# Last tile's first LayerNorm affine moved to VectorE in two halves, and the first expert's low parts and index work re-ordered

## The chip, the cores and the metric

The kernel runs on one core of a Trainium2 chip. The metric is the device time of one execution in microseconds (us), as the median of several runs. Beside it stands one execution taken by the hardware profiler; all rows of the trace below are of that one.

## The reference

Two decoder layers over 512 tokens of width 1024. Each layer does a mixer (attention of two kinds), adds it to alpha times its input and normalises; then a mixture of 16 experts, adds and normalises again:

```python
x = layer_norm(ALPHA * x + mix, ln_g[l, 0], ln_b[l, 0])
ffn = routed_moe(x, router_w, router_b, moe_w_gate[l], moe_w_up[l], moe_w_down[l])
x = layer_norm(ALPHA * x + ffn, ln_g[l, 1], ln_b[l, 1])
```

The router takes a sigmoid of 16 logits, picks the best group of four experts, and in it the two best experts of each token. An expert is `(silu(x @ w_gate) * (x @ w_up)) @ w_down` with an inner width of 512, weighted by the token's gate.

## The kernel before, in words

Tokens are worked in four tiles of 128. A product in float32 is done as three products of split operands: each operand is a high part (a cast on ScalarE, line 185) and a low part (a subtraction on VectorE, line 186, or for activations 203 and 204), and `mm3` multiplies high by high, high by low and low by high. A weight tile of 1 MB is two units, each with one cast and one subtraction of 128x1024. There are four buffers for high parts and four for low parts (pool `hl`).

The stage that the diff touches lies between a layer's mixer and its experts, in `out_proj` and at the head of `moe`. `ROUTE_ORDER` gives its order: `y` is the output projection of a tile and its sums (`tile_y`), `l` its LayerNorm statistics, its router logits and its normalise (`tile_ln`), and `rab` routes the tiles a to b-1. So `r02` routes tiles 0 and 1 together, `r23` tile 2, `r34` tile 3. Routing is `choose` (lines 418 to 454, a chain of small VectorE instructions, from the sigmoid `aff` to the one-hot `O` and the mask `M`), then `slots` (matmuls at 471 and 475 count the tokens ahead of each in its expert's list; 477 and 479 on VectorE make the slot numbers `sl` and the one-hot `oh0` of expert 0), then `first_rows` (line 490: 16 matmuls per tile gather the rows of expert 0 into two PSUM banks, transposed, `ps2[0]` and `ps2[1]`, lines with ps_o and ps_s).

The normalise of a tile is on ScalarE (line 589). Its scale and bias, `affine` (lines 255 and 256), are on GpSimd, but for the last 256 columns of tile 3, which VectorE does (`LN1_DVE`). The result x1 is written to HBM twice by GpSimd's DMA queue (591 to `x1d`, from which the experts' rows are gathered, and 594 to `yd`, onto which their outputs are added).

At the head of `moe`, 16 weight tiles of 1 MB are fetched ahead by the SP queue in the order `AHEAD`, into buffers named by `slot_of`; some are those of the mixer's outputs (`eH`, `eL`, `lH`, `lL`). A later load waits until the tile that was in its buffer has been split. Then come the high and low parts of expert 0's gate weights (`g0`), `put_rows` (it splits the rows from PSUM into `gH` and `gL`, which lie in `m2`), and `after_slots`. That makes each slot's token index (`idx`, line 507, with eight masks and eight matmuls at 505 and 506), masks and transposes for the end of the layer (512 to 514), counts (517, 518), the gate weights (`weights`) and each slot's gate (527 to 529). Indirect DMAs gather the rows of the other experts (`gather`, line 1100), 96 rows each. The loop over 16 experts does the gate product, the up product, the activation, the transposes of the next expert's rows (`rows_in`, line 1111) and the down product of the expert before. Expert 1's gate product needs `rows_in(1)`, since `gH` and `gL` exist once.

The order of instructions on an engine is a scheduler's, made at compile time: by the order written, among those which it takes to be ready. `keep_in_program_order` pins an instruction behind the one written before it on its engine. `issue_after(x)` queues what its block writes on x's engine behind x. Neither adds a wait on another engine. `first` pins only while `in_order[0]` is set.

Of the kernel before, what the change touches and what calls it, by code (L numbers as in the profile page):

```python
# [9 lines left out]
F32 = mybir.dt.float32  # L10
# [6 lines left out]
ALU = mybir.AluOpType  # L17
# [24 lines left out]
AHEAD = (2, 3, 4, 0, 1, 5, 6, 8, 9, 10, 12, 13, 7, 14, 11, 15)  # L42


LN1_DVE = (0, 0, 0, 256)
# [22 lines left out]
def trunk_kernel(ctx: ExitStack, tc, x_in, even_w_in, even_b_f, even_sinks, odd_w_in,  # L68
# [344 lines left out]
    def choose(t0, t1):  # L413
# [40 lines left out]
        V.tensor_tensor(out=M[:, ts_], in0=O[:, ts_, 0, :], in1=O[:, ts_, 1, :], op=ALU.add)  # L454
# [27 lines left out]
    def first_rows(ps2, oh0, t0, t1):  # L482

        for c in range(2):
# [8 lines left out]
    def after_slots(sl, oht, flag):  # L493
# [13 lines left out]
        V.tensor_scalar(idx[:CAP], sp[:CAP, 0:NE], OOB, None, op0=ALU.add)  # L507

# [10 lines left out]
        weights()  # L519

        og = sm.tile([128, NT * 2, NE], F32, name="og", tag="gt", bufs=1)
        V.tensor_tensor(out=og, in0=O.rearrange("p t c e -> p (t c) e"),
                        in1=gates.rearrange("p t c -> p (t c)").unsqueeze(2).to_broadcast([128, 8, NE]), op=ALU.mult)
        sg = ps_t()
        for j in range(NT * 2):
            eq = sm.tile([128, CAP], F32, name="eq")
            V.tensor_scalar(eq, slot1, pos[:, j:j + 1], None, op0=ALU.is_equal)
            T.matmul(sg[:CAP, 0:NE], eq, og[:, j, :], start=(j == 0), stop=(j == NT * 2 - 1))
        A.activation(out=gslot[:CAP], in_=sg[:CAP, 0:NE], func=AF.Copy, scale=1.0 / ALPHA)
# [17 lines left out]
    def out_proj(l, chunk_src, oH, oL, g, x1d, yd, work, main):  # L547
# [35 lines left out]
        def tile_ln(i):  # L583
# [5 lines left out]
            A.activation(out=xr[i], in_=xr[i], func=AF.Identity, scale=rs, bias=minus(mv[:, 0, 0:1], rs))  # L589
            affine(xr[i], gb, bb, LN1_DVE[i])  # L590
# [11 lines left out]
        for f, *n in ROUTE_ORDER.split():  # L602
            i = int(n[0])
            if f == "y":
                tile_y(i)
            elif f == "l":
                tile_ln(i)
            else:

                j = int(n[1])  # L610
                if i == 0:
                    ps2 = [ps_o(), ps_s()]
                choose(i, j)
                slots(sl, oh0, i, j)
                first_rows(ps2, oh0, i, j)
        return sl, ps2, oht
# [433 lines left out]
    def moe(l, mo, sl, ps2, oht, x1d, yd, flag, following, finish):  # L1050
# [22 lines left out]
        def fetch(t, w, e, c, chain=False):  # L1073
# [6 lines left out]
            elif t in "eElx":  # L1080
                t = xo.tile([128, 2048], F32, name="wraw3", tag=dict(e=eH, E=eL, l=lL, x=lH)[t])
# [48 lines left out]

        def act(g, u, n=1):
# [3 lines left out]
            for j in range(n):  # L1135
                cs = slice(j * FF // n, (j + 1) * FF // n)
                V.tensor_tensor(out=sg[:, cs], in0=sg[:, cs], in1=u[j], op=ALU.mult)
# [52 lines left out]
        for c in range(2):  # L1190
# [170 lines left out]
    def layer(l, proj, x1d, yd, following, finish):  # L1361
        with tc.tile_pool(name="mo", bufs=1, reuse_waits="tile") as mo:
            sl, ps2, oht = out_proj(l, *proj, x1d, yd, mo, True)
            moe(l, mo, sl, ps2, oht, x1d, yd, flags[:, l:l + 1], following, finish)
# [42 lines left out]
```

## Time and profile before

| what | value |
|---|---|
| median of three runs | 1181.48 us (1177.25 to 1182.6) |
| profiled execution | 1180.26 us, span 1178.5 us |
| TensorE (PE) busy | 1093.0 us, 93% |
| VectorE (DVE) busy | 934.3 us, 79% |
| ScalarE (ACT) busy | 762.3 us, 65% |
| GpSimd (POOL) busy | 266.5 us, 23% |
| mean granted TensorE clock | 0.954 |

The span runs from the first to the last instruction. Times in rows are from its start. PEld is TensorE's loading of stationary operands; SP is the engine whose queue issues the weight loads, and q behind an engine's name stands for its sequencer. In a timeline a row has the start, the duration, engine, line, operation, what it writes and reads, how many alike in a row, and in brackets the idle time of the engine before it with what ended it. Layer 0's routing lies between 224 and 286 us, layer 1's between 814 and 874 us.

### The profile page before, as it was taken

To read this page: it belongs to the slowest core of one execution; us is meant where nothing else is said; L and a number is where in the kernel's file an instruction comes from. 1 tells how busy PE (TensorE), PEld (TensorE's weight loads), DVE (VectorE), ACT (ScalarE), POOL (GpSimd) and SP (SyncE) were. 2 spreads that over 40 slices of the span, in tenths; PEclk is the share of its full clock that TensorE was granted. 3 is DMA by queue.
4 is the path that set the end of the run, shared out by engine and by line. 5 is a ranking of instruction groups with operands and counts; after the bars stand their busy time and mean duration, and the time that the engine had idled before them with its cause. 6 is when DMAs were issued, how large, how long until landed. Compare 5 with 4: busy or idle time off the path is not lost. (4 is left out here: it accounts for less than half of the span.)

```text
span 1178.5 us, 16701 instructions
## 1 busy us (share of the span) xinstructions
PE 1093.0 (93%) x5775; PEld 817.5 (69%) x5775; DVE 934.3 (79%) x1866; ACT 762.3 (65%) x1229; POOL 266.5 (23%) x223
## 2 busy tenths in 40 slices
PE   8999989979999999998599898999799999999982
PEld 7786767867777777776377665777677777777761
DVE  4646756597999999987766998766879999999976
ACT  4556646235888888887435744654268888888862
POOL 2001340251111141112613133003411111411023
PEclk9999999988999999999699998999789999999997
DMA  8314332779999997998512211335699999989972
GB/s 209 117 40 90 75 88 105 255 276 303 302 358 357 350 334 237 361 357 279 183 28 72 73 37 37 107 108 209 240 299 285 365 342 353 339 255 366 371 234 108
DMA packets 139613, 262.25 MB, mean 223 GB/s; under 512 B 11831, under 2 KB 28247, under 8 KB 139520
## 3 DMA queue, kind: packets, MB, share of 16 engines
q1 hardware_dynamic: 129232, 234.62, 57.9%
q0 software_dynamic: 10288, 26.48, 9.1%
q8 instruction: 47, 0.77, 0.3%
q14 instruction: 46, 0.38, 0.1%
HBM read 246.73 MB, written 22.30 MB: 228 GB/s over the span
## 5 line engine op out<-in xcount | busy, mean ns | idle before, releaser
L186 DVE TENSOR_TENSOR wl<-wraw,wh 128x1024 fp32r<-128x1024 f32 (+1 forms) x418 | 503.6, 1231 | 83.3 <-ACT wh L185 74.9
L185 ACT CAST wh<-wraw 128x1024 fp32r<-128x1024 f32 (+3 forms) x436 | 445.7, 1039 | 155.0 <-PE ps_s L200 63.8
L198 PE MATMUL ps_s<-wh,m 128*96 128x512 f32 (+1 forms) x528 | 208.3, 394 | 1.7 <-ACT m L203 1.7
L199 PE MATMUL ps_s<-wl,m 128*96 128x512 f32 (+1 forms) x528 | 206.4, 391 | 0.0
L200 PE MATMUL ps_s<-wh,m 128*96 128x512 f32 (+1 forms) x528 | 205.0, 388 | 0.4 <-DVE m L204 0.4
L200 PEld LDWEIGHTS ps_s<-wh,m 128*96 128x96 f32 x528 | 86.4, 164 | 35.7 <-DVE m L204 1.3
L198 PEld LDWEIGHTS ps_s<-wh,m 128*96 128x96 f32 x528 | 86.7, 164 | 34.8 <-ACT m L203 2.1
L199 PEld LDWEIGHTS ps_s<-wl,m 128*96 128x96 f32 x528 | 86.4, 164 | 31.9 <-issue 0.2
L198 PE MATMUL ps_a<-wh,hH 128*96 128x512 f32 x256 | 102.7, 401 | 3.8 <-ACT hH L203 3.8
L199 PE MATMUL ps_a<-wl,hH 128*96 128x512 f32 x256 | 101.8, 398 | 4.0 <-POOL wl L186 4.0
L200 PE MATMUL ps_a<-wh,hL 128*96 128x512 f32 x256 | 101.0, 394 | 1.3 <-DVE hL L204 1.3
L198 PE MATMUL ps_a<-wh,XH 128*128 128x512 f32 (+2 forms) x224 | 89.4, 399 | 4.3 <-ACT wh L185 3.2
L1100 POOL DMA_INDIRECT m<-x1d,idx x30 | 33.1, 1104 | 255.8 <-PE ps_t L1111 224.2
L200 PE MATMUL ps_a<-wh,XL 128*128 128x512 f32 (+2 forms) x224 | 88.7, 396 | 1.9 <-DVE XL L204 1.9
L1175 POOL DMA_INDIRECT yd<-m,idx x30 | 49.2, 1640 | 177.0 <-ACT m L1174 173.3
L199 PE MATMUL ps_a<-wl,XH 128*128 128x512 f32 (+2 forms) x224 | 88.8, 396 | 0.0
L199 PE MATMUL ps_a<-XL,wh 128*128 128x512 f32 x160 | 65.0, 406 | 0.0
L200 PE MATMUL ps_a<-XH,wl 128*128 128x512 f32 x160 | 64.7, 405 | 0.3 <-DVE wl L186 0.3
L198 PE MATMUL ps_a<-XH,wh 128*128 128x512 f32 x160 | 64.6, 403 | 0.0
L357 ACT ACTIVATE p<-p,nm 128x256 f32<-128x256 f32 (+3 forms) x96 | 50.6, 529 | 17.8 <-DVE nm L350 8.8
L376 ACT COPY pT<-ps_t 128x512 f32<-128x512 f32 (+2 forms) x88 | 43.4, 517 | 28.8 <-PE ps_t L373 28.0
L199 PEld LDWEIGHTS ps_a<-wl,hH 128*96 128x96 f32 x256 | 41.3, 161 | 20.5 <-POOL wl L186 5.4
(327 smaller groups left out, 1918.3 us busy)
## 6 DMA issues: line engine op xcount, KB each, us to landing
wraw<-in_moe_w_up_dram SPq DMA_DIRECT2D x64, 1024.0 KB
wraw<-in_moe_w_gate_dram SPq DMA_DIRECT2D x64, 1024.0 KB
wraw<-in_moe_w_down_dram SPq DMA_DIRECT2D x64, 1024.0 KB
wraw<-in_w_o_dram SPq DMA_DIRECT2D x6, 1024.0 KB
wraw<-in_even_w_in_dram SPq DMA_DIRECT2D x4, 1024.0 KB
x1d<-xr POOLq DMA_DIRECT2D x8, 512.0 KB
yd<-xr POOLq DMA_DIRECT2D x8, 512.0 KB
xr<-yd SPq DMA_DIRECT2D x8, 512.0 KB
```

The source lines that it names most:

```text
L185: first(A.copy(hv, w))
L186: first(eng.tensor_tensor(out=lv, in0=w, in1=hv.bitcast(F32), op=ALU.subtract))
L198: T.matmul(o, lh, rh, start=first, stop=False)
L199: T.matmul(o, lh, rl, start=False, stop=False)
L200: T.matmul(o, ll, rh, start=False, stop=last)
L357: A.activation(out=pt[h], in_=(pt if bias else Sp)[h], func=AF.Exp, bias=nm[:, h:h + 1], scale=(slopes[0][h] if slopes else 1.0), accum_ou ...
L376: A.copy(d_, s_)
L1100: G.indirect_dma_start(out=xg_of[e], out_offset=None, in_=x1d[:, :], in_offset=bass.IndirectOffsetOnAxis(ap=idx[:CAP, e:e + 1], axis=0), b ...
L1175: G.indirect_dma_start(out=yd[:, :], out_offset=bass.IndirectOffsetOnAxis(ap=idx[:CAP, e:e + 1], axis=0), in_=yos[e % 2], in_offset=None, ...
```

## The change

Tile 3's scale and bias move from GpSimd (768 columns) and VectorE (256) to VectorE alone, in halves of 512 columns: the first behind its choice, the second behind its one-hot `oh`, where `first_rows` is split in two as well. The writes of x1 of tile 3 move behind that. The normalise of every tile is pinned behind its sigmoid. The first expert's gate weights are split behind the last one-hot and in a written order: first half, both `put_rows`, second half. What `after_slots` did for expert rows and gates is written behind the first gate product; what it did for the layer's end becomes `for_the_end`, written in expert 4 behind the activation of expert 3. Buffers change places: `m2` lies in `lL`, and `m3` and the weight tile of place 7 (expert 1's up, second half) in `eL`, whose first tenant is the second half of the first gate; that weight tile is fetched last of the 16.

```diff
-AHEAD = (2, 3, 4, 0, 1, 5, 6, 8, 9, 10, 12, 13, 7, 14, 11, 15)
+AHEAD = (2, 3, 4, 0, 1, 5, 6, 8, 9, 10, 12, 13, 14, 11, 15, 7)
-LN1_DVE = (0, 0, 0, 256)
+LN1_DVE = (0, 0, 0, 1024)
...
-    def affine(x, gb, bb, nv):
+    def affine(x, gb, bb, nv, half=None):
         for e, cs in ((G, slice(0, D - nv)), (V, slice(D - nv, D))):
-            if cs.start < cs.stop:
+            if half is not None:
+                cs = slice(half * 512, half * 512 + 512)
+            if cs.start < cs.stop and (half is None or e is V):
...
-            A.activation(out=xr[i], in_=xr[i], func=AF.Identity, scale=rs, bias=minus(mv[:, 0, 0:1], rs))
-            affine(xr[i], gb, bb, LN1_DVE[i])
+            tc.keep_in_program_order(A.activation(out=xr[i], in_=xr[i], func=AF.Identity, scale=rs, bias=minus(mv[:, 0, 0:1], rs)))
+            if i < NT - 1 or not main:
+                x1(i, True)
...
-                choose(i, j)
-                slots(sl, oh0, i, j)
-                first_rows(ps2, oh0, i, j)
+                chosen = choose(i, j)
+                if j < NT:
+                    slots(sl, oh0, i, j)
+                    first_rows(ps2, oh0, i, j)
+                    continue
+                with tc.issue_after(chosen.ins):
+                    affine(xr[i], gb, bb, D, 0)
+                oh = slots(sl, oh0, i, j)
+                first_rows(ps2, oh0, i, j, (0,))
+                with tc.issue_after(oh.ins):
+                    affine(xr[i], gb, bb, D, 1)
+                first_rows(ps2, oh0, i, j, (1,))
+                x1(i)
...
-                m3 = xo.tile([128, 2, D], F32, name="m3", tag=lL)
+                m3 = xo.tile([128, 2, D], F32, name="m3", tag=eL)
...
-        g0 = [ksplit(load("g", 0, c), 2) for c in range(2)]
-        m2 = xo.tile([128, 2, D], F32R, name="m2", tag=eL)
+        m2 = xo.tile([128, 2, D], F32R, name="m2", tag=lL)
-        for c in range(2):
-            put_rows(c, ps2[c])
-        after_slots(sl, oht, flag)
-        for e in (1, 2):
-            gather(e)
+        with tc.issue_after(oh.ins):
+            in_order[0] = True
+            g0 = [ksplit(load("g", 0, 0), 2)]
+            for c in range(2):
+                put_rows(c, ps2[c])
+            g0.append(ksplit(load("g", 0, 1), 2))
+            in_order[0] = False
         for e in range(NE):
             g = up("g", e, None if e else g0)
+            if e == 0:
+                after_slots(sl)
+                for i in (1, 2):
+                    gather(i)
+            if e == 4:
+                with tc.issue_after(act_op[0].ins):
+                    for_the_end(sl, oht, flag)
```

## Rows read from the trace of the kernel before

**Rows 1.** The page: the busy time of each engine with its share of the span and its instructions, and the share of the chain that ended last by engine.

```profile
PE 1093.0 (93%) x5775; PEld 817.5 (69%) x5775; DVE 934.3 (79%) x1866; ACT 762.3 (65%) x1229; POOL 266.5 (23%) x223
PE 24%; DVE 2%; ACT 1%; issue 0%; POOL 0%; DVEq 0%; ACTq 0%
```

**Rows 2.** The chain that ended last, in layer 1's routing and behind it, in order of time: start, us, what.

```profile
848.93 1.86 DVE xr L256
851.11 1.99 PE ps_o L490 x8
853.10 1.71 PE ps_s L490 x8
855.76 1.99 PE ps_o L490 x8
857.75 1.71 PE ps_s L490 x8
...
876.42 0.23 PE ps_s L199
```

**Rows 3.** The timeline of VectorE in layer 1's routing.

```profile
842.98 1.21 DVE L186 TENSOR_TENSOR wl<-wraw,wh 128x1024 fp32r<-128x1024 f32 x1
...
846.80 2.05 DVE L255 TENSOR_TENSOR xr<-xr,lnt 128x256 f32<-128x256 f32 x1
...
848.89 1.91 DVE L256 TENSOR_TENSOR xr<-xr,lnt 128x256 f32<-128x256 f32 x1
...
850.88 0.16 DVE L418 TENSOR_TENSOR sel<-aff,rb 128x16 f32<-128x16 f32 x1
...
853.51 0.17 DVE L454 TENSOR_TENSOR M<-O 128x16 f16<-128x16 f16 x1
...
855.36 0.26 DVE L479 TENSOR_TENSOR oh<-slot,sl 128x96 f32<-128x96 f16 x1
...
858.34 0.56 DVE L204 TENSOR_TENSOR m<-ps_o,m 128x384 fp32r<-128x384 f32 x1 [1.21 <-ACT m L203]
...
862.38 0.17 DVE L507 TENSOR_SCALAR idx<-ps_s 96x16 uint32<-96x16 f32 x1 [0.98 <-PE ps_s L506]
...
871.08 2.36 DVE L186 TENSOR_TENSOR wl<-wraw,wh 128x1024 fp32r<-128x1024 f32 x2 [1.69 <-ACT wh L185]
```

**Rows 4.** The timeline of GpSimd, four rows of layer 1's routing, then one of layer 0's.

```profile
846.77 1.80 POOL L255 TENSOR_TENSOR xr<-xr,lnt 128x768 f32<-128x768 f32 x1 [4.42 <-ACT xr L589]
848.65 1.86 POOL L256 TENSOR_TENSOR xr<-xr,lnt 128x768 f32<-128x768 f32 x1
851.33 0.59 POOL L591 DMA_DIRECT2D x1d<-xr  x1 [0.82 <-DVE eq L512]
...
862.84 1.08 POOL L1100 DMA_INDIRECT m<-x1d,idx  x1 [10.39 <-DVE eq L527]
...
264.06 0.59 POOL L591 DMA_DIRECT2D x1d<-xr  x1 [0.30 <-POOL xr L256]
```

**Rows 5.** The timeline of ScalarE in layer 1's routing: tile 3's normalise and its sigmoid.

```profile
845.45 1.24 ACT L589 ACTIVATE xr<-xr,nmr,rs_o 128x1024 f32<-128x1024 f32 x1 [4.40 <-DVE nmr L248]
846.59 0.20 ACT L588 ACTIVATE aff<-u 128x16 f32<-128x16 f32 x1
```

**Rows 6.** The timeline of TensorE in layer 1: the last of the first two tiles' rows, a transpose of a mask for the layer's end, the transposes of expert 1's rows.

```profile
844.14 3.46 PE L490 MATMUL ps_s<-oh,xr 128*128 128x96 f32 x16
847.44 0.27 PE L513 MATMUL ps_t<-ident,eq 128*96 128x128 f32 x1
...
873.18 0.82 PE L1111 MATMUL ps_t<-ident,m 96*128 96x96 f32 x8
```

**Rows 7.** The timeline of VectorE in layer 0's routing.

```profile
256.35 1.22 DVE L186 TENSOR_TENSOR wl<-wraw,wh 128x1024 fp32r<-128x1024 f32 x1
...
259.74 0.42 DVE L255 TENSOR_TENSOR xr<-xr,lnt 128x256 f32<-128x256 f32 x1
...
262.02 1.85 DVE L479 TENSOR_TENSOR oh<-slot,sl 128x96 f32<-128x96 f16 x1
```

**Rows 8.** The timeline of TensorE in layer 0: the last of the first two tiles' rows, the last of tile 3's, the transposes of expert 1's rows.

```profile
257.21 1.95 PE L490 MATMUL ps_s<-oh,xr 128*128 128x96 f32 x16
...
270.47 1.91 PE L490 MATMUL ps_s<-oh,xr 128*128 128x96 f32 x8
...
285.97 0.82 PE L1111 MATMUL ps_t<-ident,m 96*128 96x96 f32 x8
```

**Rows 9.** Windows of layer 1's routing: the stretch, its length, then busy us and instructions of PE, PEld, DVE, ACT and POOL, the granted TensorE clock, the DMA engines' busy share, and GB/s.

```profile
847.30:850.70 3.40, 0.68 (x11) 0.56 (x10) 3.40 (x3) 0.00 (x0) 3.13 (x2) 1.00 1.03 414
850.70:861.00 10.30, 9.27 (x46) 8.72 (x47) 6.65 (x39) 1.54 (x3) 1.12 (x2) 0.50 0.89 318
...
855.62:869.40 13.78, 13.64 (x74) 11.04 (x74) 10.61 (x34) 6.98 (x8) 2.24 (x2) 0.81 0.80 270
```

**Rows 10.** Windows of layer 0's experts, with the same columns.

```profile
440.00:448.00 8.00, 8.00 (x41) 5.78 (x40) 7.50 (x9) 6.85 (x10) 1.00 (x1) 1.00 0.70 226
448.00:456.00 8.00, 8.00 (x38) 5.63 (x37) 7.20 (x8) 6.89 (x10) 1.57 (x1) 1.00 0.48 121
...
472.00:544.00 72.00, 70.42 (x335) 49.99 (x334) 65.13 (x65) 60.32 (x73) 8.89 (x6) 1.00 1.04 360
```

**Rows 11.** Waits of the SP queue from 850 to 880 us: who waited for whom, us in total, times, longest.

```profile
SPq L1092 <- DMA x1d<-xr: 7.8, 1, 7.8
```

More of the change, by code (lines that the diff above doesn't have):

```diff
@@ L453, in choose @@
                         in1=f8.rearrange("p t c -> p (t c)").unsqueeze(2).to_broadcast([128, 2 * n, NE]), op=ALU.is_equal)
-        V.tensor_tensor(out=M[:, ts_], in0=O[:, ts_, 0, :], in1=O[:, ts_, 1, :], op=ALU.add)
+        return V.tensor_tensor(out=M[:, ts_], in0=O[:, ts_, 0, :], in1=O[:, ts_, 1, :], op=ALU.add)
     def weights():
@@ L480, in slots, with first_rows @@
                                in1=sl[:, t0:t1, 0:1].to_broadcast([128, n, CAP]), op=ALU.is_equal)
-    def first_rows(ps2, oh0, t0, t1):
-        for c in range(2):
+    def first_rows(ps2, oh0, t0, t1, cs=range(2)):
+        for c in cs:
             if t0 == 0:
@@ L491, in first_rows, with after_slots @@
                              oh0[:, i, :], start=False, stop=(i == NT - 1 and k == 3))
-    def after_slots(sl, oht, flag):
+    def after_slots(sl):
         Of = O.rearrange("p t c e -> p (t c) e")
@@ L507, in after_slots, with for_the_end @@
         V.tensor_scalar(idx[:CAP], sp[:CAP, 0:NE], OOB, None, op0=ALU.add)
+        weights()
+        og = sm.tile([128, NT * 2, NE], F32, name="og", tag="gt", bufs=1)
+        V.tensor_tensor(out=og, in0=O.rearrange("p t c e -> p (t c) e"),
+                        in1=gates.rearrange("p t c -> p (t c)").unsqueeze(2).to_broadcast([128, 8, NE]), op=ALU.mult)
+        sg = ps_t()
+        for j in range(NT * 2):
+            eq = sm.tile([128, CAP], F32, name="eq")
+            V.tensor_scalar(eq, slot1, pos[:, j:j + 1], None, op0=ALU.is_equal)
+            T.matmul(sg[:CAP, 0:NE], eq, og[:, j, :], start=(j == 0), stop=(j == NT * 2 - 1))
+        A.activation(out=gslot[:CAP], in_=sg[:CAP, 0:NE], func=AF.Copy, scale=1.0 / ALPHA)
+    def for_the_end(sl, oht, flag):
         p = ps_t()
@@ L518, in after_slots @@
         V.tensor_reduce(out=flag, in_=cnt[:, 0:NE], axis=AX.X, op=ALU.max)
[L519 to L529, printed above, removed]
     def half_proj(chunk, oH, oL, g, i):
@@ L588, in tile_ln, with x1 @@
                 A.activation(out=aff[:, i, :], in_=u[:, i, :], func=AF.Sigmoid)
-            A.activation(out=xr[i], in_=xr[i], func=AF.Identity, scale=rs, bias=minus(mv[:, 0, 0:1], rs))
-            affine(xr[i], gb, bb, LN1_DVE[i])
+            tc.keep_in_program_order(A.activation(out=xr[i], in_=xr[i], func=AF.Identity, scale=rs, bias=minus(mv[:, 0, 0:1], rs)))
+            if i < NT - 1 or not main:
+                x1(i, True)
+        def x1(i, whole=False):
+            if whole:
+                affine(xr[i], gb, bb, LN1_DVE[i])
             nc.gpsimd.dma_start(x1d[i * 128:(i + 1) * 128, :], xr[i])
@@ L1047, in odd_mixer, with moe @@
             return wo_src, oH, oL, 0
-    def moe(l, mo, sl, ps2, oht, x1d, yd, flag, following, finish):
+    def moe(l, mo, sl, ps2, oht, oh, x1d, yd, flag, following, finish):
         last = NE - 1
@@ L1080, in fetch @@
             elif t in "eElx":
-                t = xo.tile([128, 2048], F32, name="wraw3", tag=dict(e=eH, E=eL, l=lL, x=lH)[t])
+                t = xo.tile([128, 2048], F32, name="wraw3", tag=dict(e=eH, E=eL, l=eL, x=lH)[t])
             elif t in "01":
@@ L1129, in up @@
             return os_
+        act_op = [None]
         def act(g, u, n=1):
@@ L1136, in act @@
                 cs = slice(j * FF // n, (j + 1) * FF // n)
-                V.tensor_tensor(out=sg[:, cs], in0=sg[:, cs], in1=u[j], op=ALU.mult)
+                act_op[0] = V.tensor_tensor(out=sg[:, cs], in0=sg[:, cs], in1=u[j], op=ALU.mult)
             return sg
@@ L1362, in layer @@
         with tc.tile_pool(name="mo", bufs=1, reuse_waits="tile") as mo:
-            sl, ps2, oht = out_proj(l, *proj, x1d, yd, mo, True)
-            moe(l, mo, sl, ps2, oht, x1d, yd, flags[:, l:l + 1], following, finish)
+            sl, ps2, oht, oh = out_proj(l, *proj, x1d, yd, mo, True)
+            moe(l, mo, sl, ps2, oht, oh, x1d, yd, flags[:, l:l + 1], following, finish)
     early = []
```

3 lines of the change are left out of this document (1 added, 2 removed).

## The prediction

> **What bounds the kernel now.** I read the page first. TensorE is busy 93% of the span and VectorE 79%, and of the 27% of the span over which the chain that ended last can be followed back 24 lie on TensorE [rows 1]. So an edit pays only where TensorE stands still or runs at its lower rate, and the place that this diff touches is one: between a layer's mixer and its experts the tokens of the last tiles are routed, and every weight product of the first expert waits for that. I read that stretch of layer 1 next, first in the chain of waits, then engine by engine. The chain [rows 2] runs through the last tile's bias on VectorE (848.93, 1.86 us), then through `first_rows` of tile 2 (851.11 to 854.81) and of tile 3 (855.76 to 859.46). These 32 matmuls take 3.7 us per tile, while 16 of them at the higher rate took 1.95 in all in layer 0 [rows 8], 1.85 start to start for a tile. The windows say why: granted clock 1.00 from 847.3 to 850.7 with TensorE busy for 0.68 us only, then 0.50 until 861 [rows 9].
>
> Why TensorE stood still there is in [rows 3]. Tile 2's choice was ready at 846.8. Then VectorE did its 256 columns of tile 3's scale, 2.05 us, where the same instruction takes 0.42 in layer 0 [rows 7]: GpSimd was at its own 768 columns from 846.77 to 848.57 [rows 4]. Tile 2's slots came behind it, then the bias, 1.91 us beside GpSimd's 1.86, then tile 2's one-hot, and only at 850.88 tile 3's choice, whose input had been there since 846.8 [rows 5]. Layer 0 has the same: the one-hot of tile 2 takes 1.85 us at 262.02 [rows 7].
>
> **The change, part by part.** Times are layer 1's, then layer 0's.
>
> *The affine leaves the choice's way.* Four instructions of 512 columns replace two of 256 on VectorE and two of 768 on GpSimd. Between 0.42 (256 columns) and 1.21 (1024, a low part [rows 3]) 512 columns cost 0.69, or 1.26 for a half, since each starts 0.06 before the one ahead ends. In layer 1 TensorE ends the first two tiles' rows at 847.60 [rows 6]. From the end of one tile's rows to the start of the next lie 0.95 us (854.81 to 855.76 [rows 2]): slots, one-hot, start. So tile 2's rows can start at 848.55 instead of 851.11, if its choice is there, and it is (846.8). Tile 3's choice takes 2.80 us (850.88 to 853.68 [rows 3]). The pin of the normalise puts the sigmoid ahead of it, which saves the 1.1 us by which it stood behind [rows 5]. Two of the first gate's low parts, 1.15 us each, leave the chain of tile 3's statistics (842.98 is one, 256.35 in layer 0). So the choice is done before tile 2's rows are, and the first half of the affine lies under them.
>
> *The clock.* TensorE then has 2.5 us of work in the 3.4 us where it had 0.68 [rows 9]. I take the higher rate: rows of tile 2 from 848.55 to 850.40, of tile 3 from 851.35 to 853.20; one-hot of tile 3 done at 851.2. In layer 0 the first rows end at 259.16 [rows 8]; tile 2's rows go from 260.10 to 261.95, the one-hot is done at 262.75, tile 3's rows end at 264.75. The ends were 859.46 and 272.18 (a last piece at 270.47, 1.71 after it as in the chain). That alone is 6.3 and 7.4 us, and no more than this can be won: it is the far end of the range.
>
> *What VectorE owes afterwards.* Part of it is given back, since the low parts now stand behind the one-hot. From there VectorE has in this order: second half 1.26, two low parts 2.36, both `put_rows` 1.1 (0.56 each), two low parts 2.36 [rows 3], so 7.1 us; then the indices and gate weights, then the four low parts of the first up product, 4.72. The middle term comes from the same stretch of before: busy 10.61 us from 855.62 to 869.40 [rows 9], less four low parts, two `put_rows` and one transpose mask (0.2), leaves 4.6 us. Together 1.26 + 4.72 + 1.1 + 4.6 + 4.72 = 16.4 us. The last low part is then done at 867.6 (279.15 in layer 0), and the up product ends 1.2 us later, five matmuls at 0.23 [rows 2]: 868.8 and 280.35, against 873.18 and 285.97, when the transposes of expert 1 start now [rows 6, 8]. Gains 4.4 and 5.6. Before, VectorE stood idle for 3.2 of those 13.8 us, mostly waiting for TensorE. The queue is fuller now, so I take 0.7 us of that for each layer: 3.7 and 4.9. TensorE waits for VectorE here, not the other way round.
>
> *The rows of expert 1.* Its transposes need the gather, and that needs the indices and x1 in HBM. GpSimd issues the write of tile 3 now at 851.33 and after the change once the second half is done, at 852.5 (in layer 0 at 264.0, where it is 264.06 now [rows 4]). The SP queue waited 7.8 us for that write [rows 11], so its flight is that and the 0.5 or so that went before: it lands near 860.8. The indices need some 3 us of the 4.6 behind the 7.1: 861.3, against 862.38. The gather was issued at 862.84 and used at 873.18, with nothing waiting for it: its flight lies between its own 1.08 us [rows 4] and 10.3. It is nearest to the write, three quarters of whose rows it moves, so between 6 and 8; I take 7. Issued at 861.7 it lands at 868.7, just when VectorE lets TensorE through. At 10.3 it would land at 872 and leave 1.2 us in layer 1; both ends are in the range.
>
> The Trainium skill (SBUF — State Buffer, "SBUF: two separate sides") warns that a DMA from GpSimd's queue starves while VectorE holds the port pair that the two share. The rows do not show it here: the gather's issue at 862.84 ran beside low parts for 1.08 us. By the page's rule the write would wait out VectorE's 7.1 us; that is the third rival.
>
> *What moves out.* The masks, transposes and counts for the end go to expert 4. There TensorE is the bound, so they cost: four transposes at up to 0.27 [rows 6] less their overlap, and four small matmuls, 0.6 us a layer; nothing if the loop has a hole, 1.4 at the lower rate. Copy and masks hide under TensorE.
>
> *The weights.* The late load of the first expert-1 up tile moves to the buffer of the first gate's second half, and a down tile waits for the affine's end, 852.5 for 850.8. The later of them is issued at 858.3, and neither is needed before the second half of expert 1's up product, 8 us behind the transposes; I cost them at nothing. The cover is the DMA engines' slack: in the middle of layer 0's experts they stand at 0.70 and 0.48 for 8 us each, 6.6 us of slack, and at 1.04 behind it [rows 10]. The end of layer 0 is thus paced by transfers, and TensorE can run ahead by 5 us only because the stream takes up that slack.
>
> **Sum.** 3.7 + 4.9 - 1.2 = 7.4 us. The profiled execution took 1180.3 us (span 1178.5), so 1172.9; the median of the runs stands 1.2 above it, so I predict **1174**.
>
> **The rivals.**
> *The clock stays low.* For: it fell and took until 861 to rise, and TensorE still has two holes of about 0.9 us and one while VectorE does the first `put_rows`. Against: the granted 1.00 from 847.3. Each one-hot comes 1.85 us later: gains 1.8 and 3.0, less 1.2, gives 1177.9.
> *The transfers keep layer 0.* If the delayed loads use up the 6.6 us, the stream lands as before and layer 0's gain is lost: 3.7 - 1.2, so 1179. Against: before, the stream also waited for buffers that now come free earlier. That the reordering does not take effect, as the instructions were already in such an order, gives 1181; the rows of VectorE speak against it.
> *GpSimd's write starves.* Issued at 858.3, landed 866.6, gathered by 873.9, 0.7 later than now; layer 0 0.5 earlier. With the 1.2: 1183. The issue time above speaks against it.
> *Slower: the up product's low parts run ahead of the indices.* Both are ready together and the order between them is the scheduler's. The indices then come at 851.2 + 7.1 + 4.72 + 3 = 866.0. From a flight over 6.8 us on TensorE waits longer than before. With the bound, 10.3, layer 1 is 3.5 later and layer 0 2.2, with the 1.2 some 6.9: 1188.4. Against: the index work is written ahead of that product.
>
> **How the numbers follow.** Under 0.5% (5.9 us) this kernel's measurement cannot tell from no change. Forecast, 1170 to 1175.5: 0.50. Beyond it, down to the full 13.7 us of the rows' own gain, 1167.8: 0.07. Clock low: 0.18. Transfers, or no effect: 0.11. Starved write: 0.05. Low parts ahead: 0.09, of which 0.01 stays within 0.5%. So faster 0.57, same 0.35, slower 0.08. The range goes from 1167 to 1182: it leaves out the starved write, the late indices and a little below.
>
> **What would show it.** Right: tile 2's one-hot within 1 us of the first rows' end, at about 0.25 us in both layers; no affine on GpSimd for tile 3; clock 1.00 from 850 on; transposes of expert 1 near 869 and 281; then equal periods per expert with one longer by some 0.6; both dips of the DMA share still there. Wrong: a hole on TensorE ahead of those transposes with the gather or a low part as releaser; the sigmoid still behind the normalise; the half of the affine ahead of a one-hot (1.3 us); or last casts of layer 0 at their old times.

## The result and the profile after

The change made the kernel slower. The median of four runs is 1195.0 us (1194.5 to 1197.3), beside 1180.1 for the kernel before on the same chip: a ratio of 1.0136, with a 95% interval of 1.0112 to 1.0160. The forecast of 1174 and its range, 1167 to 1182, both missed. The profiled execution has a span of 1192.6 us, 14.1 more than before.

The page after, busy time by engine and the share of the chain that ended last, answers to [rows 1]:

```profile
PE 1093.3 (92%) x5775; PEld 814.1 (68%) x5775; DVE 941.7 (79%) x1870; ACT 762.0 (64%) x1229; POOL 265.4 (22%) x219
PE 35%; DVE 9%; ACT 2%; DMA 2%; issue 1%; POOL 1%; SPq 0%; DVEq 0%; POOLq 0%; ACTq 0%
```

TensorE has the same busy time, so the 14 us are new standing still; the mean granted clock is 0.957 (0.954 before), so what a lower clock costs in one stretch is given back in others. DVE stands in the chain with 9%, 2% before, and DMA with 2%. But the chain can be followed back over 50% of this span and over 27% of the one before, so the shares alone say little. The waits of TensorE say where the time goes, from a layer's first LayerNorm statistics to the activations of its first experts: who waited for whom, us in total, times, longest. First the kernel before, layer 0 and layer 1:

```profile
PE ps_o L490 <- DVE sel L418: 4.1, 1, 4.1
PE ps_t L576 <- DVE xr L571: 2.9, 1, 2.9
...
PE ps_o L490 <- DVE sel L418: 4.1, 2, 3.1
PE ps_t L576 <- DVE xr L571: 3.0, 1, 3.0
```

And after the change, in the same order:

```profile
PE ps_t L580 <- DVE xr L575: 5.6, 2, 3.3
PE ps_t L1131 <- DMA m<-x1d,idx: 4.0, 1, 4.0
...
PE ps_t L1131 <- DMA m<-x1d,idx: 6.0, 1, 6.0
PE ps_t L580 <- DVE xr L575: 5.7, 2, 3.3
```

The waits of 4.1 us ahead of the first rows (`ps_o`) are gone, but for some of 0.4 to 1.1. In their place stand two others. The transposes of expert 1's rows wait for the gather, 4.0 and 6.0 us: the hole that the prediction named as a sign of its being wrong. And the wait for a tile's last addition (line 575, 571 before) comes twice instead of once, 2.7 us more in each layer. VectorE in layer 1 shows both causes; the columns are those of [rows 3], and line 420 is the head of a choice (418 before), 479 the slots, 509 the indices (507 before):

```profile
842.67 1.88 DVE L420 TENSOR_TENSOR sel<-aff,rb 128x16 f32<-128x16 f32 x1
...
845.07 1.93 DVE L424 TENSOR_TENSOR pr<-sel 128x8 f32<-128x8 f32 x1
...
849.09 0.68 DVE L575 TENSOR_TENSOR xr<-xr,ps_a 128x512 f32<-128x512 f32 x1
...
854.96 0.22 DVE L435 SCALAR_TENSOR_TENSOR gs<-gs,gm,desc 128x4 f32<-128x4 f32 x1
858.79 0.17 DVE L479 SCALAR_TENSOR_TENSOR sl<-ps_s,M 128x16 f32<-128x16 f32 x1 [3.61 <-PE ps_s L477]
...
862.06 0.26 DVE L481 TENSOR_TENSOR oh<-slot,sl 128x96 f32<-128x96 f16 x1
...
863.64 2.35 DVE L186 TENSOR_TENSOR wl<-wraw,wh 128x1024 fp32r<-128x1024 f32 x2
...
867.94 2.36 DVE L186 TENSOR_TENSOR wl<-wraw,wh 128x1024 fp32r<-128x1024 f32 x2 [0.39 <-ACT wh L185]
...
870.41 1.22 DVE L186 TENSOR_TENSOR wl<-wraw,wh 128x1024 fp32r<-128x1024 f32 x1
...
873.69 1.19 DVE L186 TENSOR_TENSOR wl<-wraw,wh 128x1024 fp32r<-128x1024 f32 x1
874.80 0.17 DVE L509 TENSOR_SCALAR idx<-ps_s 96x16 uint32<-96x16 f32 x1
```

Tile 2's choice (from 842.67) now stands ahead of tile 3's last addition (849.09), for which TensorE waits. Two instructions of that choice, which take 0.16 us when alone, took 1.88 and 1.93. Tile 3's choice is begun, and then VectorE stands for 3.61 us, because the slots of tile 2 come next in its order and need matmuls that TensorE has queued behind the first rows. Behind the one-hot come the four held low parts, then two of the up product's, and only then the indices.

TensorE and GpSimd in layer 1, answering to [rows 6] and [rows 4]:

```profile
849.83 0.66 PE L580 MATMUL ps_t<-ident,xr 128*128 128x128 f32 x4 [2.37 <-DVE xr L575]
...
853.03 3.28 PE L492 MATMUL ps_o<-oh,xr 128*128 128x96 f32 x14
...
859.40 1.10 PE L492 MATMUL ps_o<-oh,xr 128*128 128x96 f32 x8 [0.65 <-DVE sel L437]
...
862.46 1.10 PE L492 MATMUL ps_o<-oh,xr 128*128 128x96 f32 x8 [0.98 <-DVE oh L481]
...
864.59 1.85 PE L492 MATMUL ps_s<-oh,xr 128*128 128x96 f32 x8
...
885.79 0.90 PE L1131 MATMUL ps_t<-ident,m 96*128 96x96 f32 x4 [6.01 <-DMA m<-x1d,idx]
...
864.26 0.53 POOL L600 DMA_DIRECT2D x1d<-xr  x1 [15.86 <-ACT m L203]
...
875.81 2.66 POOL L1120 DMA_INDIRECT m<-x1d,idx  x1 [10.50 <-ACT sg L1156]
```

The rows of a tile fill two banks with 8 matmuls each. Three of the four banks of tiles 2 and 3 do run at the higher rate, 1.10 us or less; the last one takes 1.85, at a granted clock of 0.50 from 864.5 to 866.4. The first tiles' rows pay the lower rate, too (14 matmuls in 3.28). The gather's issue alone takes 2.66 us, 1.08 before. The windows of this stretch in layer 0 (columns as in [rows 9]) show the price of the hole behind it, too: granted clock 0.73 until the activation of expert 1 (in layer 1 it is 0.71 from 885.8 to 895.7).

```profile
272.60:285.90 13.30, 12.48 (x59) 8.46 (x58) 12.30 (x28) 11.62 (x13) 3.56 (x2) 0.96 0.77 282
285.90:289.90 4.00, 0.02 (x1) 0.00 (x0) 1.53 (x4) 0.83 (x1) 1.42 (x1) 1.00 1.05 327
289.90:302.40 12.50, 12.00 (x54) 9.05 (x55) 8.26 (x12) 5.48 (x8) 1.01 (x1) 0.73 1.00 312
```

The difference of the two spans adds up, stretch by stretch, from the timelines (us; a layer's count starts at its first LayerNorm statistics, the end of the first rows is line 492's, 490 before):

| stretch | layer 0: before, after | layer 1: before, after |
|---|---|---|
| first statistics to the end of the first rows | 54.0, 54.6 | 67.7, 66.1 |
| to the transposes of expert 1's rows | 13.6, 17.3 | 13.7, 19.4 |
| to the activation of expert 1 | 9.3, 12.5 | 9.3, 9.9 |
| to the activation of expert 15 | 247.6, 248.0 | 247.2, 249.5 |

By the unrounded times that is 8.0 us in layer 0 and 7.0 in layer 1. Between the layers it is 1.0 more; the start is 0.4 and the end 1.4 shorter: 14.1 in all.

### The profile page after: what moved, and what is told of

The parts are those of the page before. It is cut to its first block, busy times and chain, and to the rows that moved or that the text cites. A ratio compares the mean times of both kernels' runs of the same rounds, so it can differ in the third digit from the quotient of the medians.

```text
span 1192.6 us, 16682 instructions
## 1 busy us (share of the span) xinstructions
PE 1093.3 (92%) x5775; PEld 814.1 (68%) x5775; DVE 941.7 (79%) x1870; ACT 762.0 (64%) x1229; POOL 265.4 (22%) x219
## 4 chain that ended last, share of the span: by engine, by line
PE 35%; DVE 9%; ACT 2%; DMA 2%; issue 1%; POOL 1%; SPq 0%; DVEq 0%; POOLq 0%; ACTq 0%
PE ps_s L198 5%; PE ps_s L199 5%; PE ps_s L200 4%; PE ps_a L198 4%; PE ps_a L200 4%; PE ps_a L199 4%; DVE sc L996 1%; PE ps_o L382 1%; PE ps_t L375 1%; DVE m L995 1%; PE ps_s L1021 1%; PE ps_t L1131 1%; DMA m<-x1d,idx 1%; DVE nm L354 1%; DMA xr<-yd 1%
## 5 line engine op out<-in xcount | busy, mean ns | idle before, releaser
L1120 POOL DMA_INDIRECT m<-x1d,idx x30 | 36.0, 1200 | 254.9 <-PE ps_t L1131 218.9
L1197 POOL DMA_INDIRECT yd<-m,idx x30 | 53.6, 1787 | 172.8 <-ACT m L1196 171.8
L359 ACT ACTIVATE p<-p,nm 128x256 f32<-128x256 f32 (+3 forms) x96 | 50.6, 529 | 17.2 <-DVE nm L352 8.7
```

Of the source, the lines that this page charges most:

```text
L359: A.activation(out=pt[h], in_=(pt if bias else Sp)[h], func=AF.Exp, bias=nm[:, h:h + 1], scale=(slopes[0][h] if slopes else 1.0), accum_ou ...
L1120: G.indirect_dma_start(out=xg_of[e], out_offset=None, in_=x1d[:, :], in_offset=bass.IndirectOffsetOnAxis(ap=idx[:CAP, e:e + 1], axis=0), b ...
L1197: G.indirect_dma_start(out=yd[:, :], out_offset=bass.IndirectOffsetOnAxis(ap=idx[:CAP, e:e + 1], axis=0), in_=yos[e % 2], in_offset=None, ...
```

## Experiments

The theory from these rows: the affine by itself does what was forecast, and the index work behind the first gate product, together with the held low parts, loses more than that. The rivals: the holes come from the gate masks ahead of expert 1's rows, or the affine itself brings nothing. Ratios are to the kernel before, measured beside each on the same chip.

**The affine alone.** The kernel before with the two halves on VectorE and x1's writes behind them.

```diff
...
+                with tc.issue_after(chosen.ins):
+                    affine(xr[i], gb, bb, D, 0)
+                oh = slots(sl, oh0, i, j)
+                first_rows(ps2, oh0, i, j, (0,))
+                with tc.issue_after(oh.ins):
+                    affine(xr[i], gb, bb, D, 1)
...
```

> The kernel before with only tile 3's scale and bias moved to VectorE in halves (behind its choice and behind its one-hot); nothing else of the change. My sum for this part: the rows of expert 0 end 3 to 6 us earlier in each layer, and with no low parts added behind the one-hot this reaches the experts: 5 to 10 us faster than before, 1170 to 1175. Rival (the routing is bound by the tile's projection and the counts on TensorE, so the affine was never the limit): within 2 us of before, 1178 to 1182.

Measured: 1173.3 us, 0.9935 (0.9908 to 0.9961). It beats both kernels, as expected, and has the lowest median of all that ran. The first rows end 50.6 us after layer 0's first statistics (54.0 before) and 65.4 after layer 1's (67.7). VectorE and TensorE in layer 1:

```profile
849.62 0.68 DVE L257 TENSOR_TENSOR xr<-xr,lnt 128x512 f32<-128x512 f32 x1
...
850.95 0.25 DVE L481 TENSOR_TENSOR oh<-slot,sl 128x96 f32<-128x96 f16 x1
...
857.91 0.17 DVE L509 TENSOR_SCALAR idx<-ps_s 96x16 uint32<-96x16 f32 x1 [0.22 <-PE ps_s L508]
...
847.50 1.10 PE L492 MATMUL ps_o<-oh,xr 128*128 128x96 f32 x8 [0.65 <-DVE pr L427]
...
851.35 1.10 PE L492 MATMUL ps_o<-oh,xr 128*128 128x96 f32 x8 [1.32 <-DVE oh L481]
852.66 2.02 PE L492 MATMUL ps_s<-oh,xr 128*128 128x96 f32 x8 [0.21 <-DVE xr L258]
```

An instruction of 512 columns takes 0.68 us, as worked out (0.69). Here, too, the last bank of the rows is slow: 2.02 us, behind the second half of the affine and at a granted clock of 0.52 from 852.6 to 854.7. The indices come 3.2 us behind the rows' end. The hole of 1.32 us is the half of the affine ahead of the one-hot, which the prediction has among its signs of being wrong; the changed kernel has it, too (0.98 at 862.46).

**Index work.** `idx_ahead` is the changed kernel with the index work and gathers written ahead of the first gate's parts; `gates_behind_rows` leaves them where the change put them and moves the gate weights behind expert 1's rows; `index_late_alone` and `half_index_late` are the kernel before and the affine alone, with all of `after_slots` and the gathers behind the first gate product:

```diff
...
-        after_slots(sl, oht, flag)
-        for e in (1, 2):
-            gather(e)
         for e in range(NE):
             g = up("g", e, None if e else g0)
+            if e == 0:
+                after_slots(sl, oht, flag)
+                for i in (1, 2):
+                    gather(i)
...
```

> The changed kernel with the index work and the first two gathers written ahead of the first gate's low parts; the gate weights stay behind the first gate product. Theory 1 (late indices: the gather of expert 1 leaves 6.3 us later in layer 0, TensorE waits 4.0 us in layer 0 and 6.0 us in layer 1 for it and then runs at the lower clock): indices near 273 us instead of 281, no wait of the transposes of expert 1 for the gather, both layers together 10 to 13 us faster than the changed kernel, so about the time of the kernel before (1180 to 1185). Theory 2 (the gate masks of the first expert, caught between the transposes, are the cost): no more than 2 to 4 us gained, 1191 to 1193. Theory 3 (the routing itself is slower and nothing behind it matters): no gain, 1195.

> The changed kernel with only the gate weights and their eight masks and matmuls written behind the transposes of expert 1; the indices stay late. Theory 2 (those masks, two buffers, held TensorE between the transposes from 290.3 to 294.1 us): some 3 us less a layer, about 1188 to 1190. Theory 1 (late indices): the hole in front of the transposes stays at 4 to 6 us a layer, and the time stays within 2 us of the changed kernel, 1193 to 1196.

> The kernel before with one thing changed: all of the index and gate work and the gathers of experts 1 and 2 are written behind the first gate product instead of ahead of it. The order on VectorE is then rows, indices behind two or three of the up product's low parts. Theory (late indices alone open the hole ahead of expert 1's transposes): the indices come 6 to 8 us after the end of the first rows instead of 2.9, TensorE waits 2 to 5 us in each layer with the gather as releaser, and the time is 6 to 12 us above the kernel before: 1187 to 1193. Rival 1 (the hole needs the held low parts too, since here the up product's low parts that run ahead make the first activation earlier): within 4 us of before. Rival 2 (it is the buffers' new places or the pin of the normalise, not the order of the indices): no change, 1179 to 1182.

> The affine in halves alone and with it the index and gate work and the gathers of experts 1 and 2 behind the first gate product, with the first gate's parts free and neither pin, new places nor moved end work. Theory (late indices alone turn a gain into a hole): VectorE's order now has the gate weights and three low parts of the up product ahead of the indices, they come 9 to 11 us after the rows' end in place of 2 to 3, TensorE waits 3 to 6 us for the gather in each layer, and the time is 0.999 to 1.006 of before. Rival (on the faster routing the first gate product covers it): 0.992 to 0.997, like the affine alone.

Measured: 1.0087 (1.0049 to 1.0124), 1.0136 (1.0095 to 1.0178), 1.0027 (1.0002 to 1.0052) and 1.0037 (1.0009 to 1.0066). `gates_behind_rows` and `half_index_late` came where their theories of late indices put them; `idx_ahead` gained 0.5% on the changed kernel instead of the 10 to 13 us of its first theory. When the gather was issued and what it did, in us behind the end of the first rows, layer 0 then layer 1 (the last two rows belong to the next experiment):

| kernel | indices | gather issued | TensorE ready | transposes |
|---|---|---|---|---|
| before | 2.9, 2.9 | 3.4, 3.4 | no wait | 13.6, 13.7 |
| affine alone | 4.6, 3.2 | 6.4, 7.6 | no wait | 15.0, 13.8 |
| changed | 8.4, 8.4 | 9.4, 9.4 | 13.3, 13.3 | 17.3, 19.4 |
| gates_behind_rows | 9.1, 8.8 | 10.1, 9.8 | 13.1, 13.0 | 18.9, 17.9 |
| index_late_alone | 7.1, 6.8 | 7.6, 7.3 | 13.4, 13.1 | 16.1, 17.9 |
| half_index_late | 8.7, 9.0 | 9.1, 9.5 | 14.1, 14.4 | 18.9, 19.2 |
| idx_ahead | 1.5, 1.1 | 7.0, 9.1 | no wait, 17.7 | 18.8, 18.0 |
| first_gate_free | 9.9, 9.7 | 10.4, 10.1 | 14.3, 14.1 | 19.3, 18.2 |
| held_parts_alone | 7.1, 7.1 | 8.2, 8.2 | no wait | 22.7, 20.7 |

Wherever the index work stands behind the first gate product, the gather is issued 7 to 10 us behind the rows, TensorE is ready 13 to 14 behind them, and a hole of 3 to 6 us lies between. The gate masks are not the cause: with them out of the way the holes are 5.8 and 4.9 us, and the time is the same. On the affine alone the late indices cost 1.0%, from 0.9935 to 1.0037, which is the whole gain and more; on the slower routing of the kernel before 0.3%, 3.7 us by the medians, less than the 6 to 12 that I expected. The longest waits of TensorE in `half_index_late`, layer 0 then layer 1 (its profiled execution was the fastest of its ten, 1174.3 us with a median of 1184.4, so it is read for the holes alone):

```profile
PE ps_t L1129 <- DMA m<-x1d,idx: 4.8, 1, 4.8
...
PE ps_t L1129 <- DMA m<-x1d,idx: 4.8, 1, 4.8
```

`idx_ahead` shows what is late next. Its indices are ready 1.1 us behind the rows, and yet the gather goes out at 9.1. The likely reason is x1's write, issued only 0.7 us ahead of the rows' end (GpSimd, layer 1):

```profile
866.36 0.53 POOL L603 DMA_DIRECT2D x1d<-xr  x1 [16.12 <-DVE oh L507]
...
876.14 2.13 POOL L1123 DMA_INDIRECT m<-x1d,idx  x1 [8.73 <-DVE gates L467]
```

Between the two lie 9.8 us; the prediction had put the write's flight at 8.3. The landing of this write is not in the trace. In the affine alone it is, in layer 0: 7.1 us behind the issue, and the gather starts 0.9 later. The gather's hole is gone (0.3 us in layer 1), but the low parts are later by the index work, and the first activation comes 14.5 and 13.2 us behind the rows instead of 8.3 and 8.4.

**The held low parts.** `first_gate_free` is the changed kernel with the first gate's parts free again, `held_parts_alone` the kernel before with them held (and with the buffers' places that this order needs).

```diff
...
+        with tc.issue_after(oh.ins):
+            in_order[0] = True
+            g0 = [ksplit(load("g", 0, 0), 2)]
+            for c in range(2):
+                put_rows(c, ps2[c])
+            g0.append(ksplit(load("g", 0, 1), 2))
+            in_order[0] = False
...
```

> The changed kernel with the first gate's casts, low parts and put_rows neither pinned nor held behind the last one-hot, so low parts run again between the statistics of tile 3; all else as changed. If the block of 7 us on VectorE behind the one-hot delays the indices, they come 4 to 6 us earlier and the time falls by 6 to 12 us, to 1183 to 1189. If instead the place of the index work behind the first gate product is what delays it (it waits for TensorE there), the indices stay near 280 us and the gain is under 3 us.

> The kernel before with the first gate's four low parts and both put_rows held behind the last one-hot in the written order, and with the buffers' new places that this order needs (m2 in lL, m3 and place 7 in eL, place 7 fetched last); the affine, the indices' place and the work for the layer's end are as before. VectorE then has 7 us ahead of the index work, and the indices should come 6 to 8 us after the end of the rows. Theory: the indices are late here too, but the first gate product is late by about as much, so the gather's hole is smaller than in the changed kernel: 2 to 7 us slower than before, 1182 to 1188. Rival (held parts free VectorE for the routing, as the prediction had it for two of them): rows end 1 to 3 us earlier in each layer and the total is 0 to 4 us below before.

Measured: 1.0095 (1.0058 to 1.0132) and 1.0160 (1.0095 to 1.0225). Freed in the changed kernel they give back 0.4%, and the two intervals overlap. The indices stay late (9.9 and 9.7 us) and the holes for the gather are 5.0 and 4.1 us, so in the changed kernel the place of the index work is enough to make them late. Held alone they cost as much as the whole change or more (the intervals overlap again), over twice the 2 to 7 us that I expected. TensorE's waits in layer 1 of `held_parts_alone`, and the row of the second one:

```profile
PE ps_t L576 <- DVE xr L571: 6.5, 2, 3.5
PE ps_t L513 <- DVE eq L512: 4.3, 1, 4.3
...
871.07 0.45 PE L513 MATMUL ps_t<-ident,eq 128*96 128x128 f32 x1 [4.29 <-DVE eq L512]
```

The first is the wait for the last addition. Over both layers it totals 10.6 to 11.3 us in the five kernels that hold the parts, and 5.9 to 6.7 in the other ten, the kernel before among them: the held parts are worth some 2.3 us a layer of this wait, since nothing else tells the two groups apart. It does not make the rows of `held_parts_alone` late: they end 54.3 and 65.3 us behind a layer's first statistics (54.0 and 67.7 before). What that kernel loses, it loses behind them: its transposes of expert 1 come 22.7 and 20.7 us after the rows, where the kernel before has 13.6 and 13.7. The second wait is new, and both layers have it: a transpose for the layer's end (line 513) stands on TensorE ahead of the first gate product, and its mask (512) on VectorE behind the seven microseconds of low parts. So the two re-orderings hang together: with the low parts held, index and end work ahead of the gate product stops TensorE, and behind it the gather is late.

**The rest.** `half_and_pin`, `half_and_places` and `half_and_end` are the affine alone with one more part of the change each, `end_work_alone` the kernel before with the end work in expert 4, `order_undone` the changed kernel with both re-orderings undone, `pin_undone` the changed kernel without the pin. The pin, the places and the end work are these lines:

```diff
+            tc.keep_in_program_order(A.activation(out=xr[i], in_=xr[i], func=AF.Identity, ...))
...
-AHEAD = (2, 3, 4, 0, 1, 5, 6, 8, 9, 10, 12, 13, 7, 14, 11, 15)
+AHEAD = (2, 3, 4, 0, 1, 5, 6, 8, 9, 10, 12, 13, 14, 11, 15, 7)
...
+            if e == 4:
+                with tc.issue_after(act_op[0].ins):
+                    for_the_end(sl, oht, flag)
```

> The affine in halves alone (0.9935 of before) and with it only the pin of the normalise behind its sigmoid. With both orders undone the changed kernel still lost 1% against the affine alone, so pin, buffers' places or end work must cost it. Theory now: the pin costs it. The sigmoid of tile 3 comes early, so VectorE's order starts tile 3's choice in the middle of tile 2's, tile 2's slots come later, and the rows of both tiles end 1 to 3 us later in each layer: 0.998 to 1.005 of before. Rival 1 (the buffers' places cost it): 0.991 to 0.996, like the affine alone. Rival 2 (the work for the end costs it): the same as rival 1 here.

> The affine in halves alone and with it only the buffers' new places: m2 in lL, m3 and the weight tile of place 7 in eL, place 7 fetched last. The order on VectorE is that of the affine alone. Theory (the pin costs the missing 1%): 0.991 to 0.996 of before, as the prediction costed the places at nothing. Rival (the places cost it: m2 in lL must wait longer for its buffer, or the later weight tile comes too late): 0.998 to 1.005, with put_rows or expert 1's up product waiting for a transfer or a buffer that they do not wait for in the affine alone.

> The affine in halves alone and with it only the work for the layer's end moved to expert 4. Theory (the pin costs the missing 1%): 0.992 to 0.998 of before; the loop of the experts is 1 to 2 us longer in each layer, of which the routing gives 0 to 1 back. Rival (the end work carries the loss): 0.999 to 1.005.

> The kernel before with one thing changed: masks, transposes and counts for the layer's end move from the routing to expert 4, behind expert 3's activation. Theory: VectorE and TensorE lose about 1 us of work in the routing, which the index work gains, and expert 4 becomes 1 us longer: within 2 us of before. Rival (the scheduler's order in the routing changes with it, since tile 3's choice then stands behind tile 2's affine): 2 to 5 us to either side, seen in the end of the first rows.

> The changed kernel with two things undone: the first gate's parts are free again, and the index and gate work and the gathers are written ahead of the first gate product, as before. What stays is the affine in halves, the pin of the normalise, the buffers' new places and the work for the end in expert 4. Theory (the two orders cost what the affine won, and more): 1172 to 1177, within 3 us of the affine alone, with the indices some 2 us after the rows' end and no wait for the gather. Rival (the buffers' places, the pin or the work for the end carry much of the loss): 1180 or more.

> The changed kernel with the pin of the normalise alone undone: the scheduler may put the normalise ahead of its sigmoid again. Theory (the pin cost 0.7% beside the affine alone, by interleaving the two last choices): 1.004 to 1.010 of before, against 1.0136 with the pin; the holes for the gather of expert 1 stay at 4 to 6 us. Rival (the pin's cost lies in the place it has beside free low parts, and in the changed kernel there is none): 1.011 to 1.016.

| kernel | ratio to before | 95% interval |
|---|---|---|
| half_and_pin | 1.0005 | 0.9977 to 1.0032 |
| half_and_places | 0.9956 | 0.9927 to 0.9985 |
| half_and_end | 0.9967 | 0.9929 to 1.0004 |
| end_work_alone | 1.0013 | 0.9979 to 1.0047 |
| order_undone | 1.0033 | 1.0006 to 1.0061 |
| pin_undone | 1.0146 | 1.0099 to 1.0193 |

`order_undone` was a miss: I expected 1172 to 1177, and it came out 1% above the affine alone. The three runs beside the affine put most of that on the pin, 0.7%; places and end work are within their intervals of nothing. But `pin_undone` shows no gain from taking the pin out of the changed kernel, so its cost belongs to the order with free low parts. In `half_and_pin` layer 0 has a wait of 1.5 us for the gather that the affine alone has not: x1's write goes out 0.7 us ahead of the rows' end instead of 1.6, and the gather at 7.3 instead of 6.4 behind it. The affine in halves leaves little room here: the write goes out 0.7 to 1.9 us ahead of the rows' end in the kernels that have it with the index work in its old place, 8.1 to 8.3 in the kernel before, and in layer 1 of `order_undone` and `half_and_end` TensorE waits 2.1 us for the gather. The rest of the 0.7% stays open; the two traces don't settle it.

The end work lengthens one period. TensorE in layer 1 of the changed kernel, experts 3, 4 and 5 (from one activation to the next):

```profile
932.50:949.80 17.30, 17.30 (x86) 12.25 (x84) 16.43 (x19) 14.71 (x18) 2.58 (x2) 1.00 1.04 363
949.80:968.50 18.70, 18.70 (x93) 13.32 (x92) 17.04 (x22) 15.98 (x21) 2.56 (x2) 1.00 1.04 351
968.50:986.20 17.70, 17.70 (x86) 12.60 (x85) 16.31 (x17) 15.10 (x19) 2.56 (x2) 1.00 0.99 336
```

The middle one is 1.0 above the steady 17.7 and the one ahead 0.4 below it: 0.6 net, as forecast. (The rest of layer 1's 2.3 us lies in expert 2, whose period is 19.3.)

## Why the prediction was wrong

*The affine* was right in sign: taken alone it brings 8.2 us by the medians. That this is near the 7.4 of the sum is luck. The sum is 13.7 us of the rows' gain less 5.1 for what VectorE owes and 1.2 for the end work, and the affine alone holds no low parts back and moves no end work. The first rows end 3.4 and 2.3 us earlier instead of 7.4 and 6.3. The table has the steps. The first two tiles' rows run at a lower rate (granted clock 0.73 in layer 0, 1.00 before; 0.57 in layer 1, 0.73 before), the half of the affine stands ahead of the one-hot of tile 3, and the last bank of its rows is slow. Up to the activation of expert 1 the profiles show 2.0 and 2.3 us gained, and 2.6 more between the layers, at a wait for a GpSimd low part that was anything from 1.8 to 5.1 us in the profiled executions, in code that no kernel touched; 2.5 are lost ahead of layer 0's routing.

| us later than in the working | affine alone: layer 0, layer 1 | changed: layer 0, layer 1 |
|---|---|---|
| the first row | 0.1, -0.3 | 2.9, 1.1 |
| from there to tile 2's rows | 1.5, 1.7 | 2.8, 1.2 |
| from there to tile 3's rows | 1.2, 1.0 | 0.4, 0.3 |
| tile 3's rows | 1.5, 1.5 | 2.2, 2.1 |
| the end of the rows | 4.3, 4.0 | 8.3, 4.7 |

*"Two of the first gate's low parts leave the chain of tile 3's statistics."* This failed. I booked their leaving as a help to tile 3's choice and left the order around them as it was. Without them tile 2's choice moved up ahead of tile 3's last addition, beside GpSimd's affine of tile 2, and TensorE waits 2.7 us longer for that addition. Later, tile 3's choice has tile 2's slots in its middle and waits 3.61 us; the affine alone has such a wait, too, of 2.61. Of the rows' gain of 7.4 and 6.3 us, nothing was left in layer 0 (0.7 later) and 1.6 in layer 1: 8.3 and 4.7 us of the miss (in layer 0 the working takes the old end 0.2 too early: by its own row it is 270.47 + 1.91 = 272.38). In the table the first row is late by the addition. That the parts cause this is shown: `held_parts_alone` has the second wait with the affine as before, and with the parts free (`first_gate_free`) the last addition starts 34.2 and 42.7 us behind a layer's first statistics instead of 37.0 and 48.8. That they cause the rest is not shown. With them free the rows end earlier in layer 1 only (62.2 us behind the first statistics instead of 66.1); in layer 0 they end at 56.0 instead of 54.6, at a granted clock of 0.54 from the first row to the last (0.72 in the changed kernel), and what decides that clock stays open.

*The clock* was right for three of the four banks of tiles 2 and 3 (1.10 us or less). It was wrong for the last: tile 3's rows took 4.0 us where the working has 1.85, since their second bank needs the second half of the affine, which follows the one-hot, and then ran at 0.50. And it left out the first two tiles, where 14 matmuls took 3.28.

*What VectorE owes.* By the sum TensorE is let through 15.6 us behind the rows, 16.3 with the 0.7 set aside for waits; it was ready at 13.3. So VectorE's low parts were not what held up these transposes, and the step hid the next one.

*"The rows of expert 1."* The second step that failed, by its flight. The indices came 8.4 us behind the rows where the working has 8.1, so the order was foreseen. The gather was issued at 9.4 (8.5), and its flight, for which I took 7 between 1.08 and 10.3, was 7.9 in layer 0 and 10.0 in layer 1; wherever TensorE waited for it, in all runs, it was between 6.8 and 10.6, mostly 8 to 10. Where TensorE did not wait it could be far shorter: 4.6 and 5.1 us to the landing in layer 0 of `half_and_end` and `half_and_places`, at most 6.2 in layer 1 of the affine alone. So 7 lay inside what the runs show, and the fault was to rest a sum on one value of a term that varies by more than a factor of two; what sets it is not shown. "Just when VectorE lets TensorE through" rested on that 7: the transposes came 1.7 and 3.8 us later than worked out, 1.0 and 3.1 beyond the 0.7. The cost behind a late gather was not counted at all: after the hole TensorE ran at 0.73 of its clock, with gate masks between the transposes, 3.2 us more in layer 0. In layer 1 it was 0.7 more at 0.71, with 42 matmuls in that stretch where layer 0 has 54, so the clock alone does not make the cost. The terms, 8.3 + 1.0 + 3.2 and 4.7 + 3.1 + 0.7, make 21.0 us; the spans miss the forecast by 21.5 (14.1 longer instead of 7.4 shorter).

*Rivals.* The slower one, late indices, had the right mechanism: low parts of the up product did run ahead of the indices (two of them), the hole came, and at the bound the two layers would have lost 5.7 us. It was too small because it kept the rows' gain. Its chance rested on "the index work is written ahead of that product", which is no order on VectorE. The starved write did not come: the write at 864.26 took 0.53 us for its issue beside low parts, and in `pin_undone`, with the same low parts behind the one-hot, the two layers' writes landed 7.3 and 7.1 us behind their issue. By the rule of the Trainium skill (SBUF — State Buffer, "SBUF: two separate sides") as the prediction read it, the write would have waited; the section says this of a VectorE operation in a two-port mode and leaves open whether it goes for low parts, which have two inputs. What did stretch is the gather's issue, from 1.08 to 2.66 us.

*The pin* was booked as a saving of 1.1 us. Beside the affine alone it cost 0.7%, in the changed kernel nothing that can be measured. *What moves out* was right at 0.6 a layer (0.8 from the activation of expert 1 to that of expert 15 in `half_and_end` beside the affine alone, in both layers), and the weights' places cost nothing that can be told from none (0.2%, within the intervals).

## What to carry to other kernels

When a step is moved later, count from its last consumer backwards: the gather had 10 us before, and where it came late its flight was mostly 8 to 10, so indices 5 us later could not be hidden; a flight that the trace bounds only from above is taken at that bound where the sum turns on it. Work that is held back has a second side: the scheduler puts something else in its old place, and the engine can wait there, as VectorE did for 3.61 us. Try the parts of a change by themselves before all at once; here one alone was worth 0.65%, and the other parts took three times that.

## What the runs showed of the hardware

A VectorE instruction of 16 columns, 0.16 us by itself, lasted until the GpSimd instruction that it met was done. These are GpSimd's two of tile 2 in layer 1 of the changed kernel, and VectorE's statistics between the two stretched instructions:

```profile
842.14 2.38 POOL L257 TENSOR_TENSOR xr<-xr,lnt 128x1024 f32<-128x1024 f32 x1 [6.49 <-ACT xr L593]
844.59 2.39 POOL L258 TENSOR_TENSOR xr<-xr,lnt 128x1024 f32<-128x1024 f32 x1
...
844.47 0.68 DVE L576 BATCH_NORM_STATS2 st<-xr 128x6 f32<-128x512 f32 x1
```

They end at 844.52 and 846.98; the two stretched instructions of the choice end at 844.55 and 847.00. The Trainium skill (SBUF — State Buffer, "SBUF: two separate sides") says that the pair of ports which the two engines share goes to one for a whole instruction; of VectorE's it names, besides two-port modes, those with two inputs in SBUF. The trace agrees: the two stretched ones have two such inputs, and the statistics, with one, took 0.68 us beside the second GpSimd instruction and 0.69 with GpSimd idle (849.80). So a small step of a chain on VectorE can cost 1.9 us beside a large one on GpSimd.

The indirect gather of 96 rows took 6.8 to 10.6 us from issue to use wherever TensorE waited for it, and 4.6 to its landing in layer 0 of `half_and_end`; the kernel before left it 10.2. The second gather of layer 0 in the changed kernel took 3.33 us for its issue alone, beside low parts on VectorE, where it was 1.16.

```profile
282.03 1.64 POOL L1120 DMA_INDIRECT m<-x1d,idx  x1 [10.62 <-DVE as__2909 L465]
283.98 3.33 POOL L1120 DMA_INDIRECT m<-x1d,idx  x1 [0.31 <-issue]
```
